# Roots by one GpSimd power with later users, and keys split for two head pairs at once, in a hybrid attention encoder

## The chip, the cores and the metric

The kernel runs on one core of one Trainium2 chip. A core has a matrix engine (TensorE, PE in the profile, with its weight loads as PEld), three engines for elementwise work (VectorE as DVE, ScalarE as ACT, GpSimd as POOL), and SyncE (SP), whose queue issues the DMA transfers here. The metric is the time of one launch in device microseconds (us); lower is better.

## What is computed

Two request groups (prompt and sample, 2048 tokens each, model width 1024, all in float32) pass through one encoder layer with the same weights:

```python
h = rms_norm(x, norm_w)
q_a, k_a, v_a, g_a, q_b, k_b, v_b, g_b = split(h @ w_in)   # 512|128|128|512|512|512|512|512
q_a, k_a = partial_rope(rms_norm(q_a, q_norm_a)), partial_rope(rms_norm(k_a, k_norm_a))
o_a = windowed_gqa_sink(q_a, k_a, v_a, sink_a) * silu(g_a)           # +-128 tokens, 8 query and 2 key heads of 64
q_b, k_b = rms_norm(q_b, q_norm_b), rms_norm(k_b, k_norm_b)
o_b = neighbourhood_attn(q_b, k_b, v_b, rpb_b) * silu(g_b)           # 8 x 16 window on a 64-wide grid, 8 heads
x = x + concat([o_a, o_b]) @ w_out
y = x + (p @ w_ple) * sigmoid(x @ w_ple_gate)
```

`rms_norm(x, g)` is `x * rsqrt(mean(x * x) + 1e-6) * g`. For the queries and keys the mean is taken over the 64 entries of a head, so a tile of 128 tokens with eight heads needs eight inverse square roots per token.

## The kernel before

Products in float32 are split into a high and a low part, each rounded for TensorE (`fp32r`), and formed as three matmuls (high x high, high x low, low x high). The splits follow one pattern: ScalarE writes the high part, VectorE (or GpSimd) subtracts it from the source and writes the low part.

There are three stages.

1. The first stage, tiles f = 0 to 31 (16 tiles of 128 tokens for each of the two request groups): `proj_a` projects group A's columns (`pk` for keys and values, 24 matmuls of 256 columns; `pq` for queries and `pg` for gates, 24 matmuls of 512 columns each); `unit_a` does the windowed attention of a tile, for each of the two key heads.
2. The second stage, f = 32 to 95, in two halves of 32 tiles: `proj_b` projects one half of group B's heads (four of eight) for one tile of a group (`pqk` for queries and keys, `pvg` for values and gates, 24 matmuls each); `unit_b` does the neighbourhood attention of four heads.
3. The third stage: the output projection, the residual, and the gated product with `p`.

`PLAN_A` and `PLAN_B` write out by hand at what fraction of a tile's projection work the pieces of the attention (scores `sc`, transposes of the probabilities `pt`, products with the values `po`, the end `fin`, the next tile's queries `prep`) stand between the projection's matmuls. The order of TensorE's instructions is pinned to this program order (`pinned`). On the other engines a planner orders the instructions, by program order as priority and by its own estimate of when an operand is ready; instructions inside `P(...)` keep their place. Each engine then takes its queue strictly in that order. In the loops of the projections, an index `i` counts the matmuls of one projection, and constants such as `PC = 6` (`roots` at matmul 6 of `pq`), `PV = 15` (`values`), `KA = 33` and `KB = 23` (`keys_a`, `keys_b`) say behind which matmul a piece is issued. The weights of TensorE lie in tiles `wa0` to `wa7` and `wb0` to `wb7`, which are loaded and split anew (L159, L160) at the change from the first to the second stage and between the second stage's halves.

What the change touches:

- `rsqrt` (L135) writes `y = v ** -0.5` for a tile `v` of n columns: two integer instructions for a first guess (L138, L140) and three Newton steps of three instructions (L143 to L145), all on VectorE. Its users: `roots` in `proj_a` (L459 to L466, n = 3: two key heads and the token's own root), the queries' part of `proj_a` (L488 to L494, n = 8), `proj_b` (L673 to L680, n = 8), and `stats_b` (twice, n = 16).
- The users of the roots: L464 scales the keys `kt` and L466 applies the rope to them with four GpSimd instructions (L451 to L454); L492 and L494 do the same for the queries `q`; L679 scales keys (`kb`) and queries (`qg`) of the second stage. `values` (L443) and the gate's tanh (L506) use the token's root as well.
- `keys_b` (L636) takes the transposed keys of four heads from PSUM, `pkt`, and splits them into `ks_b[0]` and `ks_b[1]`, one tile for each pair of heads; the high part of the pair's first head lies in partitions 0 to 63 and its low part in 64 to 127, and the other way round for the second. The scale `wk[:, 1:2]` (the product of the two norms' weights, over 8) is applied there. `prep_b` splits the queries without a scale, and `sc` in `unit_b` reads both.

Of the kernel before, what the change touches and what calls it, by code (L numbers as in the profile page):

```python
# [13 lines left out]
I32 = mybir.dt.int32  # L14
# [8 lines left out]
HD = 64  # L23
# [53 lines left out]
PC = 6  # L77
PB = (26, 30)
# [20 lines left out]
def emit(ctx, tc, io):  # L99
# [35 lines left out]
    def rsqrt(pool, v, y, n, tag):  # L135
        i2 = pool.tile([128, n], I32, tag=tag + "i", name=tag + "i")
        a = pool.tile([128, n], F32, tag=tag + "a", name=tag + "a")
        nc.vector.tensor_scalar(out=i2, in0=v.bitcast(I32), scalar1=1, scalar2=None,  # L138
                                op0=ALU.logical_shift_right)
        nc.vector.tensor_scalar(out=y.bitcast(I32), in0=i2, scalar1=-1, scalar2=0x5F3759DF,  # L140
                                op0=ALU.mult, op1=ALU.add)
        for _ in range(3):
            nc.vector.scalar_tensor_tensor(out=a, in0=y, scalar=-0.5, in1=y, op0=ALU.mult, op1=ALU.mult)  # L143
            nc.vector.tensor_tensor(out=a, in0=a, in1=v, op=ALU.mult)
            nc.vector.scalar_tensor_tensor(out=y, in0=a, scalar=1.5, in1=y, op0=ALU.add, op1=ALU.mult)  # L145
# [184 lines left out]
    def big(shape, dt, name):  # L330
        return ap.tile(shape, dt, tag="big", name=name, bufs=3)
# [89 lines left out]
    def proj_a(f):  # L421
# [35 lines left out]
        def roots():  # L457
# [4 lines left out]
            rsqrt(ap, vr[:, 8:11], y[:, 8:11], 3, "rqk")  # L462
# [4 lines left out]
        if f < 2:  # L467
            roots()
        yield 0, False
        pq = ptile([128, 512], "pj", "pq")  # L470
        for i, c in enumerate(project(pq, xr, lambda k, b: w_q[k][:, b, :], 215)):
            if i - 4 in HN and f in last:
                square(f + 1, HN[i - 4])
            if i == PC and f > 1:
                roots()
            if i == PV:
                values()
# [5 lines left out]
            if i == ka:  # L483
# [6 lines left out]
        rsqrt(ap, vr[:, 0:8], y[:, 0:8], 8, "rqa")  # L490
        q = ap.tile([128, 8, HD], F32, tag="qg", name="q", bufs=6)
        nc.vector.tensor_tensor(out=q, in0=pq.rearrange("p (h d) -> p h d", d=HD),  # L492
                                in1=y[:, 0:8].unsqueeze(2).broadcast_to([128, 8, HD]), op=ALU.mult)
        rope(q, 8, 0)  # L494
        yield 0, False
        pg = ptile([128, 512], "sc" if f == 1 else "pj", "pg")
        for i, c in enumerate(project(pg, xr, lambda k, b: w_g[k][:, b, :], 215)):
            if i in HG and f > 0 and not early:
                split(f + 1, HG[i])
            if i in HN and f > 0 and f not in last:  # L500
                square(f + 1, HN[i])
            yield c
# [54 lines left out]
    def stats_b(s):  # L557
# [4 lines left out]
        rsqrt(ap, ms_b[:, c], rs_b[:, c], NT, "rsb")  # L562
# [73 lines left out]
    def keys_b(kt, b, cb):  # L636
# [3 lines left out]
        for i in range(2):  # L640
            for e in range(2):
                a, z = 64 * e, 64 - 64 * e
                hi, lo = (ks_b[i][p:p + 64, 8 * b:8 * b + 8, e, 16 * cb:16 * cb + 16].rearrange("p r c -> p c r")
                          for p in (a, z))
                nc.scalar.activation(hi, pkt[a:a + 64, i], AF.Copy, scale=wk[a:a + 64, 1:2])  # L645
                nc.vector.scalar_tensor_tensor(out=lo, in0=pkt[a:a + 64, i], scalar=wk[a:a + 64, 1:2],  # L646
                                               in1=hi.bitcast(F32), op0=ALU.mult, op1=ALU.subtract)

    def proj_b(f):
# [5 lines left out]
        if not ks_b:  # L655
            ks_b.extend(big([128, 32, 2, 64], F32R, f"ks_b{i}") for i in range(2))
# [18 lines left out]
        rsqrt(ap, vr, y, 8, "rqb")  # L675
        qg = ap.tile([128, 2, 4, HD], F32, tag="qg", name="qg", bufs=6)
        kt = ap.tile([128, 4, HD], F32, tag="kt", name="kb", bufs=2)
        for dst, c in ((kt, 4), (qg[:, 0], 0)):
            nc.vector.tensor_tensor(out=dst, in0=pk[:, 64 * c:64 * c + 256].rearrange("p (h d) -> p h d", d=HD),  # L679
                                    in1=y[:, c:c + 4].unsqueeze(2).broadcast_to([128, 4, HD]), op=ALU.mult)  # L680
# [28 lines left out]
    def prep_b(f):  # L709
# [6 lines left out]
        for e in range(2):  # L716
            a, z = 64 * e, 64 - 64 * e
            nc.scalar.copy(q1[e][a:a + 64], pqt[a:a + 64])
            nc.vector.tensor_tensor(out=q2[e][a:a + 64], in0=pqt[a:a + 64], in1=q1[e][a:a + 64].bitcast(F32),
# [530 lines left out]
```

## Time and profile before

| | before |
|---|---|
| median of 3 runs | 2525.07 us (2524.78 to 2525.31) |
| the profiled execution | 2525.68 us, of which the span from first to last instruction is 2523.8 us |
| mean granted TensorE clock | 0.996 of full speed |
| busy time | PE 2478.9, PEld 2090.0, DVE 1948.5, ACT 1445.0, POOL 582.5 us |
| chain that ended last | PE 86%, DVE 6%, DMA 3%, ACT 3% |

Times in the views are in us from the span's start unless marked ns. A row of a stretch (`700.00:900.00 200.00, ...`) has, for each of PE, PEld, DVE, ACT and POOL, the busy time and in brackets the number of instructions, then the granted clock of PE (1.00 is full speed), the share of DMA engines in use and GB/s. A row of a group has line, engine, operation, what it writes and reads, the shapes, the count, then total busy us and mean ns of one, then the engine's idle time before these instructions and what ended it. A row of the timeline has start, duration, engine, line and operation, and in square brackets the idle time before it and the instruction that ended it. A row of the chain of waits has start, length, engine, what was written, and line. The first stage ends near 785 us, the second near 1870, the third takes the rest.

### The profile page before, as it was taken

Reading aid. Unit: us, or ns where it says so; the run is one execution under the profiler, and the core shown is the slowest. Engines: PE = TensorE matmul, PEld = TensorE weight load, DVE = VectorE, ACT = ScalarE, POOL = GpSimd, SP = SyncE. Lnnn points to the kernel's source line nnn. Section 1 sums busy time; section 2 is a strip of 40 time slices with the busy share of each in tenths; the row PEclk is TensorE's granted clock in tenths of the full one; section 3 lists DMA queues with packets and bytes.
Section 4 is the critical chain, followed back from the end, with each engine's and each line's share of the span. In section 5 each row is a group of like instructions: output and inputs, shape, how many; then the busy total and the mean of one; then the engine's idle time right before and its main releaser. Section 6 shows DMA issues by size and latency. Waiting matters only on the chain.

```text
span 2523.8 us, 41360 instructions
## 1 busy us (share of the span) xinstructions
PE 2478.9 (98%) x12912; PEld 2090.0 (83%) x12912; DVE 1948.5 (77%) x5860; ACT 1445.0 (57%) x3469; POOL 582.5 (23%) x873
## 2 busy tenths in 40 slices
PE   8999999999989999999999999999999999999998
PEld 7888888888877888888788888888787888888887
DVE  7888888888887777787888777787746655687776
ACT  6666666666665566666666666666864222354433
POOL 3333233323323333333333333332110000000000
PEclk9999999999999999999999999999999999999999
DMA  5333332211143555555755655455867455756764
GB/s 200 98 102 109 108 88 95 64 53 62 57 101 121 167 171 177 183 166 167 235 160 180 191 160 168 147 158 185 267 230 265 160 181 171 266 176 221 235 228 154
DMA packets 236044, 405.40 MB, mean 161 GB/s; under 512 B 30864, under 2 KB 85264, under 8 KB 230416
## 3 DMA queue, kind: packets, MB, share of 16 engines
q1 hardware_dynamic: 235824, 402.75, 50.0%
q8 instruction: 103, 1.69, 0.3%
q14 instruction: 117, 0.96, 0.1%
HBM read 297.79 MB, written 122.70 MB: 167 GB/s over the span
## 4 chain that ended last, share of the span: by engine, by line
PE 86%; DVE 6%; DMA 3%; ACT 3%; issue 1%; POOL 0%; SPq 0%; DVEq 0%; ACTq 0%; POOLq 0%
PE pqk L212 13%; PE pvg L212 13%; PE acca L1082 12%; PE accc L1082 9%; PE pq L212 6%; PE pg L212 6%; PE scb L212 3%; PE ptb L215 3%; PE pob L212 3%; PE sc L212 3%; PE pk L212 3%; PE po L212 3%; PE pt L215 3%; PE pple L212 3%; ACT s L243 1%
## 5 line engine op out<-in xcount | busy, mean ns | idle before, releaser
L243 ACT ACTIVATE s<-s,nm 128x384 f32<-128x384 f32 (+4 forms) x512 | 307.3, 601 | 341.9 <-DVE nm L238 213.9
L212 PE MATMUL pvg<-wb,xr 128*128 128x512 f32 x1536 | 462.0, 408 | 0.0
L212 PE MATMUL pqk<-wa,xr 128*128 128x512 f32 x1536 | 444.7, 412 | 0.0
L212 PEld LDWEIGHTS pqk<-wa,xr 128*128 128x128 f32 x1536 | 267.7, 190 | 37.7
L212 PEld LDWEIGHTS pvg<-wb,xr 128*128 128x128 f32 x1536 | 268.4, 190 | 31.5
L308 POOL TENSOR_TENSOR xr<-stx,xr 128x512 fp32r<-128x512 f32 x190 | 245.1, 1297 | 187.0 <-ACT xr L307 180.4
L1064 ACT CAST opd<-raw 128x512 fp32r<-128x512 f32 x224 | 131.2, 619 | 261.8 <-PE acca L1082 112.8
L1065 DVE TENSOR_TENSOR opd<-raw,opd 128x512 fp32r<-128x512 f32 x224 | 146.3, 685 | 111.8 <-ACT opd L1064 111.8
L212 PE MATMUL pg<-wb,xr 128*128 128x512 f32 x768 | 231.8, 409 | 0.0
L212 PE MATMUL pq<-wa,xr 128*128 128x512 f32 x768 | 219.9, 400 | 2.2 <-DVE wa L160 1.6
L1082 PE MATMUL accc<-opd,wb 128*128 128x512 f32 x768 | 177.0, 389 | 1.9 <-DVE r L1126 1.9
L1082 PE MATMUL acca<-opd,wa 128*128 128x512 f32 x768 | 175.9, 389 | 0.4 <-DVE opd L1065 0.4
L1082 PE MATMUL acca<-opd,s 128*128 128x512 f32 x768 | 175.8, 389 | 0.2 <-DVE opd L1065 0.2
L798 POOL TENSOR_TENSOR o_tb<-otb 128x256 f32<-128x256 f32 x64 | 48.1, 751 | 547.2 <-DVE otb L791 466.8
L1082 PEld LDWEIGHTS accc<-opd,wb 128*128 128x128 f32 x768 | 144.1, 188 | 32.2 <-DVE r L1126 2.3
L1082 PEld LDWEIGHTS acca<-opd,wa 128*128 128x128 f32 x768 | 144.0, 188 | 30.9 <-DVE opd L1065 0.9
L1082 PEld LDWEIGHTS acca<-opd,s 128*128 128x128 f32 x768 | 144.0, 188 | 30.7 <-DVE opd L1065 0.9
L212 PEld LDWEIGHTS pq<-wa,xr 128*128 128x128 f32 x768 | 139.1, 188 | 25.5 <-DVE wa L160 3.3
L212 PEld LDWEIGHTS pob<-p_t,vw 128*128 128x128 f32 (+2 forms) x832 | 133.0, 190 | 30.9 <-DVE p_t L772 6.4
L227 DVE CUSTOM_DVE_ANT_0 s<-scb,bias 128x288 f32<-128x288 f32 (+3 forms) x256 | 141.3, 553 | 18.8 <-PE scb L212 15.8
L212 PEld LDWEIGHTS pg<-wb,xr 128*128 128x128 f32 x768 | 137.8, 189 | 20.4
L646 DVE SCALAR_TENSOR_TENSOR ks_b<-pktb,wk,ks_b 64x128 fp32r<-64x128 f32 x256 | 115.1, 450 | 43.9 <-ACT ks_b L645 33.4
(170 smaller groups left out, 5256.0 us busy)
## 6 DMA issues: line engine op xcount, KB each, us to landing
stx<-x_b SPq DMA_DIRECT2D x128, 256.0 KB
vw<-v_d SPq DMA_DIRECT2D x112, 256.0 KB
stx<-x_a SPq DMA_DIRECT2D x64, 256.0 KB
stn<-x_n SPq DMA_DIRECT2D x64, 256.0 KB
v_d<-vb SPq DMA_DIRECT2D x64, 256.0 KB
ple_d<-ev SPq DMA_DIRECT2D x64, 256.0 KB
xres<-x_r SPq DMA_DIRECT2D x64, 256.0 KB
x_d<-r SPq DMA_DIRECT2D x64, 256.0 KB
```

The costliest lines, as they stand in the source:

```text
L212: pinned(nc.tensor.matmul(out, lhsT, rhs, start=start, stop=stop))
L215: pinned(nc.tensor.transpose(out, in_, eye))
L227: nc.vector.tensor_tensor_reduce(out=s[:, :n], in0=ps[:, :n], in1=bias, scale=1.0, scalar=-3.0e38, op0=ALU.add, op1=ALU.max, accum_out=sm[ ...
L243: ex = nc.scalar.activation(ss[i][:, :n], ss[i][:, :n], AF.Exp, bias=nm[:, i:i + 1], accum_out=den[:, i:i + 1])
L308: low.tensor_tensor(out=lo, in0=raw, in1=hi.bitcast(F32), op=ALU.subtract)
L646: nc.vector.scalar_tensor_tensor(out=lo, in0=pkt[a:a + 64, i], scalar=wk[a:a + 64, 1:2], in1=hi.bitcast(F32), op0=ALU.mult, op1=ALU.subtract)
L798: nc.gpsimd.tensor_tensor(out=o_t, in0=got["ot"][:, :, 0], in1=got["ot"][:, :, 1], op=ALU.add)
L1064: P(nc.scalar.copy(hi, v))
L1065: P(nc.vector.tensor_tensor(out=lo, in0=v, in1=hi.bitcast(F32), op=ALU.subtract))
L1082: pinned(nc.tensor.matmul(ps, w[k][:, a, c:c + 128], o[:, b], start=i in (0, 1, 4) and k == 0 and j == 0, stop=k == 3 and j == 2, skip_gro ...
```

## The change

`rsqrt` becomes one GpSimd instruction, a power with the exponent -0.5 from a constant tile. The instructions that use the roots move into functions of their own, which are issued later in the tile: the first stage's keys 7 matmuls behind the roots (`PW`), the first stage's queries and the second stage's keys and queries at matmul 10 of the next projection (`PR`; at matmul 1 for the last but one tile of a stretch, `last`). In the first two tiles they stay directly behind the roots. In the second stage, `ks_b` is ordered by the head's place in its pair instead of by pair, so that one copy and one subtraction split that head's keys of both pairs; the scale moves from the keys to the queries in `prep_b`.

```diff
+PW = 7
+PR = 10
...
-    def rsqrt(pool, v, y, n, tag):
-        i2 = pool.tile([128, n], I32, tag=tag + "i", name=tag + "i")
-        a = pool.tile([128, n], F32, tag=tag + "a", name=tag + "a")
-        nc.vector.tensor_scalar(out=i2, in0=v.bitcast(I32), scalar1=1, scalar2=None,
-                                op0=ALU.logical_shift_right)
-        nc.vector.tensor_scalar(out=y.bitcast(I32), in0=i2, scalar1=-1, scalar2=0x5F3759DF,
-                                op0=ALU.mult, op1=ALU.add)
-        for _ in range(3):
-            nc.vector.scalar_tensor_tensor(out=a, in0=y, scalar=-0.5, in1=y, op0=ALU.mult, op1=ALU.mult)
-            nc.vector.tensor_tensor(out=a, in0=a, in1=v, op=ALU.mult)
-            nc.vector.scalar_tensor_tensor(out=y, in0=a, scalar=1.5, in1=y, op0=ALU.add, op1=ALU.mult)
+    power = cp.tile([128, 1], F32, tag="power", name="power")
+    nc.vector.memset(power, -0.5)
+
+    def rsqrt(v, y, n):
+
+        nc.gpsimd.tensor_tensor(out=y, in0=v, in1=power.broadcast_to([128, n]), op=ALU.pow)
...
-            rsqrt(ap, vr[:, 8:11], y[:, 8:11], 3, "rqk")
+            rsqrt(vr[:, 8:11], y[:, 8:11], 3)
+
+        def keys():
+
             nc.vector.tensor_scalar_mul(y[:, 11:12], y[:, 10:11], 0.5)
             nc.vector.tensor_tensor(out=kt[:, 0:2, :], in0=pk[:, 0:128].rearrange("p (h d) -> p h d", d=HD),
                                     in1=y[:, 8:10].unsqueeze(2).broadcast_to([128, 2, HD]), op=ALU.mult)
             rope(kt[:, 0:2, :], 2, 1)
         if f < 2:
             roots()
+            keys()
...
             if i == PC and f > 1:
                 roots()
+            if i == PC + PW and f > 1:
+                keys()
...
-        rsqrt(ap, vr[:, 0:8], y[:, 0:8], 8, "rqa")
+        rsqrt(vr[:, 0:8], y[:, 0:8], 8)
         q = ap.tile([128, 8, HD], F32, tag="qg", name="q", bufs=6)
-        nc.vector.tensor_tensor(out=q, in0=pq.rearrange("p (h d) -> p h d", d=HD),
-                                in1=y[:, 0:8].unsqueeze(2).broadcast_to([128, 8, HD]), op=ALU.mult)
-        rope(q, 8, 0)
+
+        def queries():
+
+            nc.vector.tensor_tensor(out=q, in0=pq.rearrange("p (h d) -> p h d", d=HD),
+                                    in1=y[:, 0:8].unsqueeze(2).broadcast_to([128, 8, HD]), op=ALU.mult)
+            rope(q, 8, 0)
+        if f < 2:
+            queries()
...
+            if i == PR and f > 1:
+                queries()
...
-        for i in range(2):
-            for e in range(2):
-                a, z = 64 * e, 64 - 64 * e
-                hi, lo = (ks_b[i][p:p + 64, 8 * b:8 * b + 8, e, 16 * cb:16 * cb + 16].rearrange("p r c -> p c r")
-                          for p in (a, z))
-                nc.scalar.activation(hi, pkt[a:a + 64, i], AF.Copy, scale=wk[a:a + 64, 1:2])
-                nc.vector.scalar_tensor_tensor(out=lo, in0=pkt[a:a + 64, i], scalar=wk[a:a + 64, 1:2],
-                                               in1=hi.bitcast(F32), op0=ALU.mult, op1=ALU.subtract)
+        for e in range(2):
+            a, z = 64 * e, 64 - 64 * e
+            hi, lo = (ks_b[e][p:p + 64, 8 * b:8 * b + 8, :, 16 * cb:16 * cb + 16].rearrange("p r i c -> p i c r")
+                      for p in (a, z))
+            nc.scalar.copy(hi, pkt[a:a + 64])
+            nc.vector.tensor_tensor(out=lo, in0=pkt[a:a + 64], in1=hi.bitcast(F32), op=ALU.subtract)
...
-        rsqrt(ap, vr, y, 8, "rqb")
+        rsqrt(vr, y, 8)
...
-        for dst, c in ((kt, 4), (qg[:, 0], 0)):
-            nc.vector.tensor_tensor(out=dst, in0=pk[:, 64 * c:64 * c + 256].rearrange("p (h d) -> p h d", d=HD),
-                                    in1=y[:, c:c + 4].unsqueeze(2).broadcast_to([128, 4, HD]), op=ALU.mult)
+        def normed():
+
+            for dst, c in ((kt, 4), (qg[:, 0], 0)):
+                nc.vector.tensor_tensor(out=dst, in0=pk[:, 64 * c:64 * c + 256].rearrange("p (h d) -> p h d", d=HD),
+                                        in1=y[:, c:c + 4].unsqueeze(2).broadcast_to([128, 4, HD]), op=ALU.mult)
...
+            if i == (PR if f not in last else 1):
+                normed()
             yield c
...
-            nc.scalar.copy(q1[e][a:a + 64], pqt[a:a + 64])
-            nc.vector.tensor_tensor(out=q2[e][a:a + 64], in0=pqt[a:a + 64], in1=q1[e][a:a + 64].bitcast(F32),
-                                    op=ALU.subtract)
+            nc.scalar.activation(q1[e][a:a + 64], pqt[a:a + 64], AF.Copy, scale=wk[a:a + 64, 1:2])
+            nc.vector.scalar_tensor_tensor(out=q2[e][a:a + 64], in0=pqt[a:a + 64], scalar=wk[a:a + 64, 1:2],
+                                           in1=q1[e][a:a + 64].bitcast(F32), op0=ALU.mult, op1=ALU.subtract)
...
-                   ks_b[h // 2][:, r0:r0 + nr, h % 2, c0:c0 + ncol], j == 0, j == 1)
+                   ks_b[h % 2][:, r0:r0 + nr, h // 2, c0:c0 + ncol], j == 0, j == 1)
```

More of the change, by code (lines that the diff above doesn't have):

```diff
@@ L13 @@
 F32R = mybir.dt.float32r
-I32 = mybir.dt.int32
 AF = mybir.ActivationFunctionType
@@ L561, in stats_b @@
         nc.vector.tensor_scalar(out=ms_b[:, c], in0=ms_b[:, c], scalar1=EPS, scalar2=None, op0=ALU.add)
-        rsqrt(ap, ms_b[:, c], rs_b[:, c], NT, "rsb")
+        rsqrt(ms_b[:, c], rs_b[:, c], NT)
         nc.vector.tensor_scalar_mul(hr_b[:, c], rs_b[:, c], 0.5)
@@ L655, in proj_b @@
         if not ks_b:
-            ks_b.extend(big([128, 32, 2, 64], F32R, f"ks_b{i}") for i in range(2))
+            ks_b.extend(big([128, 32, 2, 64], F32R, f"ks_b{e}") for e in range(2))
         w_qk, w_vg = w_b[half]
```

## The prediction

> **What bounds the kernel now.** I read the page first (engine shares, then the chain that ended last), then the busy time of each engine in stretches of some 200 us.
>
> ```profile
> span 2523.8 us, 41360 instructions
> PE 2478.9 (98%) x12912; PEld 2090.0 (83%) x12912; DVE 1948.5 (77%) x5860; ACT 1445.0 (57%) x3469; POOL 582.5 (23%) x873
> PE 86%; DVE 6%; DMA 3%; ACT 3%; issue 1%; POOL 0%; SPq 0%; DVEq 0%; ACTq 0%; POOLq 0%
> 0.00:100.00 100.00, 90.30 (x483) 77.15 (x484) 80.65 (x297) 64.20 (x159) 32.76 (x68) 1.00 0.47 158
> 100.00:300.00 200.00, 200.00 (x1158) 176.03 (x1157) 172.56 (x659) 135.35 (x363) 64.77 (x121) 1.00 0.33 107
> 700.00:900.00 200.00, 190.08 (x944) 155.59 (x943) 154.55 (x508) 119.04 (x287) 60.75 (x73) 0.97 0.46 134
> 900.00:1100.00 200.00, 200.00 (x1094) 168.05 (x1092) 158.18 (x514) 125.02 (x306) 66.93 (x80) 1.00 0.55 172
> 1100.00:1300.00 200.00, 193.22 (x1033) 161.17 (x1032) 160.74 (x485) 130.32 (x310) 67.39 (x80) 0.98 0.61 192
> 1700.00:1900.00 200.00, 194.22 (x1032) 160.74 (x1031) 129.36 (x361) 136.57 (x313) 33.51 (x49) 1.00 0.69 225
> ```
>
> PE (TensorE) is busy for 2478.9 of 2523.8 us and makes 86% of the chain. The stretches say where the other 44.9 us lie. In the middle of the first stage (100 to 300 us) and of the second (900 to 1100 us) PE is busy in all 200.00 us: there nothing that VectorE (DVE), ScalarE (ACT) or GpSimd (POOL) does faster can move the end. PE stands idle at the start (9.70 us), at the change from first to second stage (9.92 us of 700 to 900), at the second stage's change of weights (6.78 us of 1100 to 1300) and at its end (5.78 us of 1700 to 1900), 32.2 us together. The first and the third row of these four also hold a clock of 0.97 and 0.98, so PE's work is slower there as well. What the change can win lies in these places, about 22 us of idle time behind 700 us and a little at the start. Two finer stretches and five waits of PE show who is late there.
>
> ```profile
> 720.00:730.00 10.00, 5.80 (x30) 4.28 (x28) 9.91 (x17) 7.06 (x14) 2.61 (x2) 0.86 0.75 237
> 730.00:740.00 10.00, 9.93 (x41) 8.26 (x42) 5.64 (x19) 6.79 (x17) 2.17 (x3) 0.79 0.23 64
> 726.64 0.62 PE L212 MATMUL sc<-ks_a,q 128*128 128x384 f32 x2 [1.75 <-DVE pr L605]
> 730.08 1.01 PE L212 MATMUL sc<-ks_a,q 128*128 128x384 f32 x2 [2.52 <-DVE mx L227]
> 1256.86 1.11 PE L212 MATMUL pob<-p_t,vw 128*128 128x256 f32 x4 [3.29 <-DVE q L719]
> 1274.78 0.66 PE L215 MATMUL ptb<-rowwise,s 128*128 128x128 f32 x4 [1.33 <-ACT s L243]
> 1780.31 0.67 PE L212 MATMUL pob<-p_t,vw 128*128 128x256 f32 x4 [1.10 <-DVE q L719]
> ```
>
> From 720 to 730 us PE works 5.80 us while VectorE works 9.91 us: the new weights are split on VectorE, and the scores (`sc`) wait 1.75 and 2.52 us for it. The clock then falls to 0.86 and 0.79. At 1256.86, 1274.78 and 1780.31 the waits (3.29, 1.33 and 1.10 us) end on VectorE's `q`, on ScalarE's exponentials and on `q` again. So VectorE's queue is the second limit, in a few places only.
>
> **The roots: what goes.** Each root is a chain of eleven VectorE instructions (two on integers, three times three of Newton). The groups of its middle instruction carry the price of all:
>
> ```profile
> L144 DVE TENSOR_TENSOR rqba<-rqba,vrb 128x8 f32<-128x8 f32 x192 | 32.0, 166 | 5.2
> L144 DVE TENSOR_TENSOR rqaa<-rqaa,vr 128x8 f32<-128x8 f32 x96 | 17.2, 179 | 1.2
> L144 DVE TENSOR_TENSOR rqka<-rqka,vr 128x3 f32<-128x3 f32 x96 | 15.4, 161 | 3.0
> ```
>
> Ninety-six and 192 are three per root, so there are 64 roots `rqb`, 32 `rqa` and 32 `rqk`. That is 11 x (64 x 0.166 + 32 x 0.179 + 32 x 0.161) = 237 us of 1948.5 us of VectorE, 12%, nearly all in the first 1765 us. In the full stretches this is hidden behind PE and worth nothing.
>
> **The roots: what comes.** 130 powers on POOL, on 3, 8 or (twice) 16 columns. No row shows a power. The nearest rows are products on POOL and one longer pass.
>
> ```profile
> L451 POOL TENSOR_TENSOR r<-q,tab 128x128 f32<-128x128 f32 x32 | 14.8, 463 | 248.3 <-DVE q L492 243.7 <-DVE den L252 4.6
> L453 POOL TENSOR_TENSOR r<-kt,tab 128x16 f32<-128x16 f32 x32 | 7.2, 224 | 0.0
> L798 POOL TENSOR_TENSOR o_tb<-otb 128x256 f32<-128x256 f32 x64 | 48.1, 751 | 547.2 <-DVE otb L791 466.8 <-issue 80.4
> ```
>
> A product takes 224 ns on 16 columns and 463 ns on 128: 2.1 ns a column on some 190 ns. The lower bound of a power is thus 0.21 us; it can't be below nothing, as an instruction is added. If a power is eleven passes as on VectorE, each an instruction of 224 ns, it is 2.5 us: my upper bound from rows. The ends are a factor of twelve apart; the nearest row is the short product (same engine and kind, few columns), but a power needs more steps per column, so I take their geometric mean, 0.7 us. 130 x 0.7 = 91 us on POOL, which is busy 582.5 us (23%): there is room.
>
> A rule that speaks against the change stands in the Trainium skill, GPSIMD Engine Reference, section "Performance versus the Vector engine": the same elementwise work is about twice as slow on GpSimd, and VectorE is the place for it. By that rule a root would be an estimated 2 x 1.9 = 3.8 us on POOL and the sum would come out slower, near 2550. The rows here agree only in part: POOL's 16 columns at 224 ns stand against 8 on VectorE at 166 ns, and the rule speaks of the same steps, which a power needn't be.
>
> **The users, and the wait that is added.** `kt`, `q`, `kb` and `qg` now wait on VectorE for POOL. Behind them in VectorE's queue stand the score sums, the splits of `p_t` and `pr`, and PE waits for those. What time a power has is seen in one tile of each stage.
>
> ```profile
> 207.67 0.23 DVE L459 TENSOR_SCALAR vr<-ssq,ee 128x2 f32<-128x2 f32 x1
> 210.28 0.29 DVE L464 TENSOR_TENSOR kt<-pk,y 128x128 f32<-128x128 f32 x1
> 191.59 0.22 DVE L488 TENSOR_SCALAR vr<-ssq,ee 128x8 f32<-128x8 f32 x1
> 196.85 0.69 DVE L492 TENSOR_TENSOR q<-pq,y 128x512 f32<-128x512 f32 x1
> 193.36 0.48 PE L212 MATMUL pg<-wb,xr 128*128 128x512 f32 x1
> 934.03 0.23 DVE L673 TENSOR_SCALAR vrb<-ssqb,ep_b 128x8 f32<-128x8 f32 x1
> 937.48 0.43 DVE L679 TENSOR_TENSOR kb<-pqk,yb 128x256 f32<-128x256 f32 x1
> 939.02 0.76 POOL L798 TENSOR_TENSOR o_tb<-otb 128x256 f32<-128x256 f32 x1 [9.36 <-DVE otb L791]
> ```
>
> First stage, keys: the variance is ready at 207.90 and the chain lets `kt` start at 210.28, so 2.4 us are free before anything is later than now. First stage, queries: ready at 191.81, `q` starts at 196.85; the eleventh matmul of `pg` (the new place) starts at 193.36, and the 1.9 us of chain that are gone from the queue pay for a wait up to about 195.2, so 3.4 us. Second stage: ready at 934.26, `kb` starts at 937.48, so 3.2 us. POOL is idle for 9.36 us before 939.02, so the power doesn't queue there. At 0.7 us, even at 2.3 us, nobody is late. `qg` moves up from behind the gate's product to the place of `kb`; both finish earlier than now. The rope's four POOL instructions move with their user by at most 3 us, past one product of the gate on POOL's queue, and its transposes come a tile later; no DMA moves, so SP's queue stays. For the first two tiles the users stand right behind the power: four powers of 0.7 us take the place of chains of 1.9 us.
>
> **The keys split for both pairs.** Per tile four ACT and four VectorE instructions on 64x128 become two of each on 64x256, without the scale; the queries' split takes the scale instead.
>
> ```profile
> L645 ACT ACTIVATE ks_b<-pktb,wk 64x128 fp32r<-64x128 f32 x256 | 124.8, 487 | 30.2 <-DVE ks_b L646 24.2 <-PE pktb L215 4.3
> L646 DVE SCALAR_TENSOR_TENSOR ks_b<-pktb,wk,ks_b 64x128 fp32r<-64x128 f32 x256 | 115.1, 450 | 43.9 <-ACT ks_b L645 33.4
> L718 ACT CAST q1b<-pqtb 64x256 fp32r<-64x256 f32 x128 | 46.1, 360 | 47.0 <-DVE q L719 44.8 <-PE pqtb L215 2.0
> L719 DVE TENSOR_TENSOR q<-pqtb,q1b 64x256 fp32r<-64x256 f32 x128 | 53.6, 419 | 3.4 <-ACT q1b L718 1.2
> L694 ACT ACTIVATE vb<-pvg,rs_b 128x256 fp32r<-128x256 f32 x64 | 30.5, 477 | 17.9 <-PE pvg L212 17.8
> ```
>
> The plain 64x256 forms take 360 (L718) and 419 ns (L719), but write in a row; L645 and L646 write strided. A merged one costs between 360 and 2 x 487 ns on ACT, between 419 and 2 x 450 ns on VectorE; I take the middle, 0.67 and 0.66 us, so each pair saves 0.30 and 0.24 us. The scale costs a query's split about 477 - 360 = 0.12 us on ACT (L694 has one, at the same 256 columns); I take as much for VectorE. Over 128 of each: ACT 23 us less (bounds 64 less, 15 more), VectorE 15 us less (bounds 46 less, 15 more). The scores' matmuls read `ks_b` in the same row stride as before, so PE's work stays.
>
> **The sum.** Only the places with idle PE count. Here the chain of waits, in order of time, is needed for the change of stages (first and last of seventeen pieces of root chains between them, 2.0 us in all, and the weights behind), then PE's first wait and the exponentials' last input near 1273.
>
> ```profile
> 701.94 0.07 DVE rqaa L143
> 714.52 0.09 DVE y L145
> 714.92 4.35 DMA wa<-w_in_c
> 5.87 1.96 PE L212 MATMUL pk<-wx,xr 128*128 128x256 f32 x6 [5.87 <-ACT wx L159]
> 1273.14 0.73 DVE L238 TENSOR_SCALAR nm<-mx 128x4 f32<-128x4 f32 x1
> ```
>
> - Start: of the 9.70 us the first weights hold 5.87, which stay. The first two tiles lose four chains; of the other 3.8 us I give them 1 us.
> - First to second stage: the 2.0 us of root chains on the path go, and the transfer of the weights, which begins behind them, comes earlier; the splits behind it stay. With a shorter stall the clock falls less, about 1 us: 3 us.
> - Change of weights near 1250: the exponentials before 1274.78 wait for `nm` at 1273.14, in front of which seven instructions of a root chain lie between weight splits: of 7 x 0.166 = 1.2 us I count 0.8, since neighbours overlap; merged keys and the earlier `qg` take about 1.2 us from the wait of 3.29 us and its neighbours, the clock 0.5 us: 2.5 us.
> - End of the second stage: merged keys and `qg`, 1 us.
> - Elsewhere 0; the last 600 us hold no root.
>
> 1 + 3 + 2.5 + 1 = 7.5 us. The profiled execution took 2525.68 us (span 2523.8 and 1.9 around it), 0.6 us above the median of 2525.07. 2525.07 - 7.5 = 2517.6, say 2518. A measurement of this kernel spreads by 0.02%; I count a change of under 0.2% (5 us) as none.
>
> **The rivals.**
> *Nothing moves.* PE's stalls are set by weights that land late (the chain ends them with DMA and weight splits), so VectorE's free time lies elsewhere. For it: most of the 12% is in stretches with 200.00 us of PE. Against: VectorE is at 9.91 of 10 us in the worst one. Time: 2525, between 2521 and 2529. Chance 0.22.
>
> *The power is longer than its gap.* VectorE takes its queue in order; a power of 8 columns above 3.2 us makes it stand, and PE after it. At 4.0 us a second-stage tile loses up to 4.0 - 3.2 = 0.8 us, 64 x 0.8 = 51 us, and a first-stage tile 4.0 - 3.4 = 0.6, 32 x 0.6 = 19 us; the power on 3 columns is shorter, 0.19 + 3/8 x 3.8 = 1.6 us, and stays under its 2.4. Half of these 70 us are absorbed, since VectorE has 20% idle time: 2525 + 35 = 2560; at 3.5 us only some 10 us are left, at 6 us over 100. For it: no row bounds a power from above with certainty, and each column may be worked out in software. Against: 2.5 us for eleven separate passes is still under the gap. Chance 0.28. The Trainium skill's rule on GpSimd, above, points to this rival.
>
> **How the numbers follow.** The forecast has 0.50; its own range is 2511 (stalls and clock dips nearly gone) to 2524 (1 us won). Three quarters of it lie below 2520, the rest within 0.2%. Faster: 0.50 x 0.75 + 0.02 of the first rival = 0.40. Same: 0.125 + 0.18 + the short end of the second rival = 0.31. Slower: 0.29, nearly all of it the second rival. The range 2511 to 2550 holds the forecast but for its tail, the first rival and some 40% of the second, 0.8 together.
>
> **What would show it.** Right: POOL shows 130 powers of under 2.4 us; VectorE's busy time falls by 230 to 290 us; few waits of `kt`, `q`, `kb` for POOL; PE's busy share in 700 to 900 rises and the clock there stays above 0.97; 100 to 300 and 900 to 1100 keep 200.00. Wrong: powers above 3 us with VectorE waiting for them in every tile (second rival), or the same idle time of PE at the same weight splits (first rival). A new order of VectorE's queue, which a planner writes, could also shift single waits by a few us either way; that is in the ranges.

## The result, and the profile after

| | before | after |
|---|---|---|
| median | 2525.19 us (2524.78 to 2529.02, 4 runs) | 2593.98 us (2591.05 to 2594.53, 4 runs) |
| the profiled execution | 2525.68 us | 2594.49 us, span 2592.7 us |
| mean granted TensorE clock | 0.996 | 0.994 |

The changed kernel is slower: its time is 1.0267 times that of before, 95% interval 1.0249 to 1.0284. That lies outside the forecast's range (2511 to 2550). First the page and the stretches of the changed kernel (for each engine the busy time and the number of instructions):

```profile
span 2592.7 us, 39712 instructions
PE 2506.2 (97%) x12912; PEld 2086.1 (80%) x12912; DVE 1731.8 (67%) x4303; ACT 1412.8 (54%) x3341; POOL 774.8 (30%) x1003
PE 56%; DVE 13%; ACT 9%; POOL 8%; issue 7%; DMA 6%; SPq 0%; POOLq 0%; DVEq 0%; ACTq 0%
0.00:100.00 100.00, 85.61 (x441) 72.82 (x441) 61.49 (x183) 58.30 (x141) 42.58 (x71) 0.95 0.47 156
100.00:300.00 200.00, 193.09 (x1098) 167.13 (x1097) 144.67 (x445) 129.98 (x351) 80.91 (x134) 1.00 0.30 96
700.00:900.00 200.00, 192.51 (x980) 159.00 (x979) 134.28 (x362) 116.71 (x285) 80.67 (x93) 0.99 0.41 119
900.00:1100.00 200.00, 193.91 (x1036) 157.66 (x1036) 125.52 (x327) 115.12 (x272) 87.53 (x92) 1.00 0.55 169
```

VectorE (DVE) lost 217 us of work, and still the two stretches that were full have gaps: 193.09 and 193.91 of 200 us. The number of matmuls tells it more clearly than the busy share. From 100 to 300 us there are 1098 where there were 1158; 5.2% fewer, worth 10.4 us of that stretch. From 900 to 1100 there are 1036 where there were 1094. VectorE has 13% of the chain (before 6%) and GpSimd (POOL) 8% (before nothing). The groups and waits name the cause (the waits have total us, times, longest):

```profile
L141 POOL TENSOR_TENSOR yb<-vrb,power 128x8 f32<-128x8 f32 x64 | 106.1, 1658 | 212.7 <-DVE vrb L680 199.7
L141 POOL TENSOR_TENSOR y<-vr,power 128x8 f32<-128x8 f32 x32 | 52.8, 1651 | 106.9 <-DVE vr L490 106.9
L141 POOL TENSOR_TENSOR y<-vr,power 128x3 f32<-128x3 f32 x32 | 27.6, 862 | 71.1 <-DVE vr L455 71.1
DVE kb L688 <- POOL yb L141: 80.9, 61, 1.8
DVE q L497 <- POOL y L141: 35.7, 29, 2.7
DVE y L462 <- POOL y L141: 32.1, 31, 1.3
PE sc L208 <- DVE mx L223: 25.0, 28, 1.9
PE pob L208 <- DVE p_t L783: 18.4, 55, 0.8
```

The row of the kernel before for the same wait for score maxima:

```profile
PE sc L212 <- DVE mx L227: 4.6, 5, 2.5
```

A power takes 1.65 us on 8 columns and 0.86 us on 3, under the gaps of 3.2, 3.4 and 2.4 us that the prediction read. Even so VectorE stands 149 us for it, in nearly every tile, and TensorE waits for score maxima (`mx`, 25.0 us; before 4.6) and split probabilities (`p_t`, 18.4 us; before 2.4). The two timelines of VectorE's queue around a root show how that fits together. The first is before, behind the queries' variance that ends at 191.81 us and the second stage's that ends at 934.26:

```profile
192.39 0.55 DVE L227 CUSTOM_DVE_ANT_0 s<-sc,mask 128x384 f32<-128x384 f32 x1
194.21 0.16 DVE L145 SCALAR_TENSOR_TENSOR y<-rqaa,y 128x8 f32<-128x8 f32 x1
195.57 0.56 DVE L227 CUSTOM_DVE_ANT_0 s<-sc,mask 128x384 f32<-128x384 f32 x1
...
935.78 0.17 DVE L143 SCALAR_TENSOR_TENSOR rqba<-yb 128x8 f32<-128x8 f32 x1
935.87 0.68 DVE L227 CUSTOM_DVE_ANT_0 s<-scb,bias 128x512 f32<-128x512 f32 x1
936.59 0.17 DVE L238 TENSOR_SCALAR nm<-mx 128x4 f32<-128x4 f32 x1
```

The second shows the changed kernel: a later tile of the first stage with the same shapes, and the same tile of the second stage:

```profile
400.09 0.22 DVE L490 TENSOR_SCALAR vr<-ssq,ee 128x8 f32<-128x8 f32 x1
400.40 1.65 POOL L141 TENSOR_TENSOR y<-vr,power 128x8 f32<-128x8 f32 x1 [3.43 <-DVE vr L490]
402.08 0.69 DVE L497 TENSOR_TENSOR q<-pq,y 128x512 f32<-128x512 f32 x1 [1.17 <-POOL y L141]
402.69 0.55 DVE L223 CUSTOM_DVE_ANT_0 s<-sc,mask 128x384 f32<-128x384 f32 x1
403.30 0.61 PE L208 MATMUL sc<-ks_a,q 128*128 128x384 f32 x2 [0.82 <-DVE mx L223]
404.96 0.56 DVE L223 CUSTOM_DVE_ANT_0 s<-sc,mask 128x384 f32<-128x384 f32 x1
...
968.90 0.23 DVE L680 TENSOR_SCALAR vrb<-ssqb,ep_b 128x8 f32<-128x8 f32 x1
970.89 0.42 DVE L688 TENSOR_TENSOR kb<-pqk,yb 128x256 f32<-128x256 f32 x1 [1.16 <-POOL yb L141]
971.23 0.68 DVE L223 CUSTOM_DVE_ANT_0 s<-scb,bias 128x512 f32<-128x512 f32 x1
971.96 0.17 DVE L234 TENSOR_SCALAR nm<-mx 128x4 f32<-128x4 f32 x1
```

Before, the gap was not empty. The planner had woven the score sums (L227) between the eleven instructions of the chain: in the first stage the first sum began 0.58 us behind the variance and the fourth 3.76 us, in the second stage the fourth sum 1.61 us and the negated maximum `nm` 2.33 us. After the change there is nothing to weave into: `q` or `kb` stands in the queue ahead of sums, VectorE waits idle at it, and the sums behind it (four in the first stage, the fourth in the second) wait as well. In the first stage the first sum now begins 2.38 us behind the variance (402.69 - 400.31) and the fourth 4.65 us, 1.8 and 0.9 us later than before. TensorE waits 0.82 us at 403.30. In the second stage the fourth sum begins 2.10 and `nm` 2.83 us behind the variance, 0.5 us later each. This tile is a mild one: over the 55 tiles of the second stage in which two sums follow the variance, the median place of `nm` moves from 1.87 to 2.67 us behind it. And the users stand directly behind the root although they are issued seven and ten matmuls later, since the planner places what is not pinned by its own estimate of when an operand is ready.

### The profile page after: what moved, and what is told of

Read it like the earlier page. It is cut to its first block, busy times and chain, and to the rows that moved or that the text cites. A ratio compares the mean times of both kernels' runs of the same rounds, so it can differ in the third digit from the quotient of the medians.

```text
span 2592.7 us, 39712 instructions
## 1 busy us (share of the span) xinstructions
PE 2506.2 (97%) x12912; PEld 2086.1 (80%) x12912; DVE 1731.8 (67%) x4303; ACT 1412.8 (54%) x3341; POOL 774.8 (30%) x1003
## 4 chain that ended last, share of the span: by engine, by line
PE 56%; DVE 13%; ACT 9%; POOL 8%; issue 7%; DMA 6%; SPq 0%; POOLq 0%; DVEq 0%; ACTq 0%
PE acca L1093 12%; PE accc L1093 9%; PE pq L208 6%; PE pvg L208 4%; PE pqk L208 4%; PE pg L208 4%; PE pk L208 3%; PE po L208 3%; PE pple L208 3%; POOL yb L141 2%; PE sc L208 2%; ACT s L239 2%; PE pt L211 2%; POOL xr L304 2%; POOL y L141 2%
## 5 line engine op out<-in xcount | busy, mean ns | idle before, releaser
L141 POOL TENSOR_TENSOR yb<-vrb,power 128x8 f32<-128x8 f32 x64 | 106.1, 1658 | 212.7 <-DVE vrb L680 199.7
L208 PE MATMUL pob<-p_t,vw 128*128 128x256 f32 (+7 forms) x832 | 133.2, 273 | 27.5 <-DVE p_t L783 18.4
L802 DVE TENSOR_TENSOR otb<-pob,otb 64x512 f32<-64x512 f32 x128 | 88.1, 688 | 100.4 <-ACT otb L801 97.5
```

The lines of the kernel that those rows point to most:

```text
L141: nc.gpsimd.tensor_tensor(out=y, in0=v, in1=power.broadcast_to([128, n]), op=ALU.pow)
L208: pinned(nc.tensor.matmul(out, lhsT, rhs, start=start, stop=stop))
L802: nc.vector.tensor_tensor(out=ot[a:a + 64], in0=pq[a:a + 64], in1=ot[a:a + 64], op=ALU.add)
```

## The experiments

**Theory 1 (T1):** VectorE stands in its queue for the power, with score sums behind it. **Rivals:** the new splits cost (T2), or GpSimd's load and what it shares (T3). All ratios are to the kernel before, measured beside each run; the brackets are 95% intervals.

**The parts.** The first run has the new split of keys alone, the second all but it, the third VectorE's chain again under the later users and the new split.

```diff
 # e1_keys_only: kernel before, and of the change only keys_b, prep_b and the operand of sc
-                nc.scalar.activation(hi, pkt[a:a + 64, i], AF.Copy, scale=wk[a:a + 64, 1:2])
+            nc.scalar.copy(hi, pkt[a:a + 64])
...
 # e2_no_keys: changed kernel, and these hunks undone
...
 # e8_chain_late: changed kernel, rsqrt with the eleven VectorE instructions of before
-        nc.gpsimd.tensor_tensor(out=y, in0=v, in1=power.broadcast_to([128, n]), op=ALU.pow)
+        nc.vector.tensor_scalar(out=i2, in0=v.bitcast(I32), scalar1=1, scalar2=None, ...
```

> The kernel before with only the second stage's keys split for both pairs at once (and the scale moved to the queries); the roots stay on VectorE. Theory 1 (the loss is VectorE standing in its queue for the power, 1.0 to 1.3 us at each of 128 roots, with the score sums behind it): 2520, between 2515 and 2527, since this part has no power. Theory 2 (the loss comes from the longer split of the queries and the new shapes of the key split in the second stage): 2555 or more. Theory 3 (the loss comes from POOL's 192 us of powers, which hold POOL and the SBUF interface that it shares with VectorE): 2525.

> The changed kernel with the key split as it was before; powers and later users stay. Theory 1: 2595 to 2602, as slow as the changed kernel or a little slower, with 1.0 to 1.3 us of VectorE's idle time before each kb, q and kt. Theory 2: about 2555, half of the loss gone. Theory 3: 2595.

> The changed kernel with its roots by VectorE's chain of eleven instructions again; the later users and the new split of keys stay. Theory 1 (only the wait for the power costs): as with the split of keys alone, 2531 us (2524 to 2536), and VectorE's busy time near 1950 us. Rival (the moved users cost by themselves, since the second stage's queries now stand ahead of the score sums): 2540 us or more.

Measured: 1.0016 (1.0006 to 1.0025), 2531.42 us; 1.0210 (1.0194 to 1.0225), 2580.93 us; and 1.0012 (1.0003 to 1.0021), 2532.23 us. The power with its users makes 2.1 of the 2.67%. The split alone is slightly slower where T1 expected 2515 to 2527, and without it the changed kernel is faster than T1's 2595 to 2602: two misses with one reason, T1 had taken the split as free. It makes 4 us by itself and about 14 on top of the powers (2.67% against 2.10%), so T2 has a small part of the loss.

**The price of the root.** A product in place of the power (the roots are then not computed), and a second power ahead of each.

```diff
 # e4_cheap_root
-        nc.gpsimd.tensor_tensor(out=y, in0=v, in1=power.broadcast_to([128, n]), op=ALU.pow)
+        nc.gpsimd.tensor_tensor(out=y, in0=v, in1=power.broadcast_to([128, n]), op=ALU.mult)
 # e6_double
+        nc.gpsimd.tensor_tensor(out=extra, in0=v, in1=power.broadcast_to([128, n]), op=ALU.pow)
         nc.gpsimd.tensor_tensor(out=y, in0=v, in1=power.broadcast_to([128, n]), op=ALU.pow)
```

> The changed kernel with a product in place of the power (same operands, same engine, same place in the queue; the roots' values are not computed). Theory 1: the wait falls with the instruction's time, 1.65 to about 0.2 us: 2515 to 2530. Theory 2: 2590. Theory 3: 2525 as well, as POOL's busy time falls by some 165 us; e3 tells 1 from 3.

> The changed kernel with one more power of the same columns, written to a tile that nobody reads, ahead of each power. Theory 1 (the length of the power is what VectorE stands for): between a product of 0.2 us and the power of 1.65 us the time rose by 77 us for 1.45 us, 53 us for each us; a second power makes the wait 1.65 us longer, so some 88 us more, 2680 us (2650 to 2720), less if VectorE's spare time is not used up, and the waits of kb for POOL go from 1.3 to 3 us each. Rival (what costs is that an instruction of another engine stands in the chain at all, whatever its length): under 2610 us. Rival (the load on GpSimd and what it shares): the rise is as large in the stretches in which no user waits.

Measured: 0.9961 (0.9949 to 0.9974), 2516.88 us; and 1.0962 (1.0944 to 1.0981), 2773.56 us. The product's group and two stretches of its kernel, then the powers and two of TensorE's waits in the doubled one:

```profile
L141 POOL TENSOR_TENSOR yb<-vrb,power 128x8 f32<-128x8 f32 x64 | 13.8, 216 | 230.6 <-DVE vrb L680 220.7 <-DMA stx<-x_b 4.5 <-DMA raw<-w_out 3.1
100.00:300.00 200.00, 200.00 (x1161) 175.64 (x1160) 150.45 (x462) 136.36 (x364) 65.83 (x136) 1.00 0.33 105
900.00:1100.00 200.00, 200.00 (x1097) 168.04 (x1095) 131.27 (x345) 121.04 (x286) 71.05 (x95) 1.00 0.58 177
```

```profile
L144 POOL TENSOR_TENSOR yb<-vrb,power 128x8 f32<-128x8 f32 x64 | 104.9, 1639 | 0.0
PE sc L211 <- DVE mx L226: 64.1, 29, 2.5
PE ptb L214 <- ACT s L242: 63.5, 57, 1.5
100.00:300.00 200.00, 182.95 (x977) 157.96 (x976) 127.64 (x403) 115.97 (x311) 90.86 (x134) 0.94 0.27 86
1500.00:1700.00 200.00, 180.75 (x953) 145.13 (x952) 116.91 (x308) 106.35 (x253) 94.55 (x95) 1.00 0.51 156
```

With a root of 0.2 us both stretches are full again, and the kernel beats the one before: the same order of work on VectorE, ScalarE and GpSimd, the same number of GpSimd instructions, only shorter. From there to the power, 96 roots grow by 1.44 us and 32 by 0.67, 160 us in all, and the time by 3.06%, 77 us: half is absorbed. The second power adds 1.64 and about 0.85 us, 185 us, and the time grows by 6.95%, 176 us: 95% arrives at the end. Part of the second rise is TensorE's clock, 0.94 to 0.95 from 100 to 700 us, where the changed kernel had 1.00. The second stage, with 0.98 to 1.00 from 900 us on, is the cleaner measure: from its first `pqk` matmul to its last it takes 1016.5 us with the product, 1060.1 with one power and 1154.4 with two, so 47% of the first power's 92 us arrive there and 90% of the second's 105. The expected 2680 (2650 to 2720) was too low, because it went on with the first slope, when the slack was mostly used up, and because of the clock. In 57 of 64 second-stage tiles TensorE now waits for the exponentials `s`, which wait for `nm`, behind the fourth sum, behind `kb`.

**The place in the queue.** The changed kernel with users issued at once (both distances 0), then with users pinned to their written places, then pinned and with the old split.

```diff
 # e5_early
-PW = 7
-PR = 10
+PW = 0
+PR = 0
 # e3_pinned (also q, kt and the factor at L462); e7_pinned_old_keys: the same with the old split of keys
-                nc.vector.tensor_tensor(out=dst, in0=pk[:, 64 * c:64 * c + 256].rearrange(...), ...)
+                P(nc.vector.tensor_tensor(out=dst, in0=pk[:, 64 * c:64 * c + 256].rearrange(...), ...))
```

> The changed kernel with both distances set to 0: each user is issued directly behind its root in program order, as before the change. Theory 1 (VectorE stands in its queue for the power, because the planner puts the users right behind the root whatever matmul they are issued at): VectorE's queue is nearly the same one, so 2594 us, within 8. Rival (the seven and ten matmuls do carry part of the wait): the waits of q, kt and kb for POOL grow beyond the 149 us they have in the changed kernel, and the time is 2605 us or more.

> The changed kernel with the users of the roots (the factor 0.5, kt, q, kb, qg) held in program order, which puts q and kb behind the tile's four score sums in VectorE's queue instead of between them; powers, places 7 and 10 and all work stay the same. Theory 1: most of the loss goes, 2520 to 2540, VectorE's idle time before kb and q falls from 117 us to under 20 us and PE's waits for mx (25 us) to under 5 us. Theory 2: 2590. Theory 3: 2590, as POOL does the same.

> The changed kernel with its users kept at their written places in VectorE's queue and with the split of keys of the kernel before. Theory 1 with the split as an own cost: pinned it was 2538 with the new split; the new split alone costs 4 us on the kernel before and 13 us on top of the powers, so 2525 to 2534. Rival (the rest of the pinned kernel's loss comes from the pinned users, which now hold up q and kb): stays at 2538, with PE still waiting for kb at the transposes.

Measured: 1.0285 (1.0270 to 1.0301), 2602.17 us; 1.0041 (1.0026 to 1.0056), 2538.30 us; 1.0027 (1.0017 to 1.0038), 2537.48 us. Without the seven and ten matmuls the time is the same within the intervals and the waits for GpSimd are 153 us in place of 149, so these distances did nearly nothing (T1 had 2594 within 8 us, its rival 2605 or more). Pinned, most of the loss is gone at the same powers: the waits of `kb` fall from 80.9 to 5.2 us, while GpSimd is busy as long as in the changed kernel (772.5 and 774.8 us). That refutes T3, which expected 2590. The old split gives back 0.14%, within the overlap of the two intervals: e7_pinned_old_keys lies outside the 2525 to 2534 of T1 and where its rival had it, and TensorE still waits 7.1 us for `kb` in ten tiles.

```profile
L141 POOL TENSOR_TENSOR yb<-vrb,power 128x8 f32<-128x8 f32 x64 | 106.0, 1657 | 237.0 <-DVE vrb L680 231.7
DVE kb L688 <- POOL yb L141: 5.2, 3, 1.7
```

**What the pinned kernel still lost.** The chain of eleven for the first two tiles and the 16 columns; and, beside it, two parts of the kernel before by themselves: a shorter chain, and only the scale moved to the queries.

```diff
 # e10_chain_start: e7_pinned_old_keys, and in rsqrt
+        if not late:                      # f < 2, and stats_b
+            return newton_root(v, y, n)   # the eleven VectorE instructions
 # e9_two_steps: kernel before
-        for _ in range(3):
+        for k, c in ((-0.5005962965370867, 1.5017504289868662), (-0.4995838204565647, 1.4995842805920157)):
 # e11_scale_on_queries: kernel before, prep_b of the change, and in keys_b
-                nc.scalar.activation(hi, pkt[a:a + 64, i], AF.Copy, scale=wk[a:a + 64, 1:2])
+                nc.scalar.copy(hi, pkt[a:a + 64, i])
```

> The changed kernel with pinned users and the old split of keys, and with VectorE's chain of eleven instructions for the roots of the first two tiles and for the two roots of 16 columns. Theory (what the pinned kernel still loses lies at the start, where users stand directly behind powers of 0.86 and 1.65 us and TensorE works 86.7 of the first 100 us instead of 90.3, at a clock of 0.95): the loss of 0.27% halves at least, to 0.00 to 0.13% above the kernel before, and the first 100 us have 90 us of TensorE again. Rival (the loss lies in the pinned order itself, at kb and the transposes of the keys behind it): still 0.2 to 0.3% above.

> The kernel before, with two Newton steps instead of three, their constants fitted to the first guess (the worst root is then off by 6 parts in ten million); nothing waits for another engine, no place moves. Eight VectorE instructions a root instead of eleven: 65 us less of VectorE. Theory 1 (VectorE's time counts only in the places where it is late; without any power, and with the new split of keys, 84 us less of the chain's instructions per 2517 gave 11 us): about 3/11 of what the product in place of the root won, 2 to 4 us under the kernel before. Rival (the forecast's first rival, nothing moves): within 1 us of it.

> The kernel before with the scale moved from the keys' split to the queries' split, and the keys still split pair by pair in four copies and four subtractions. It is one half of the new split of keys, which as a whole cost 0.16% and 0.12%. Theory (the longer queries' split, 0.47 and 0.48 us instead of 0.36 and 0.42, delays the scores' operands): the whole cost is here, 0.10 to 0.20% above the kernel before. Rival (the merged splits cost, being longer single instructions in front of others): within 0.05%.

Measured: 1.0011 (1.0002 to 1.0020), 2532.38 us; 0.9995 (0.9986 to 1.0004), 2526.03 us; 1.0006 (0.9997 to 1.0015), 2528.83 us. The start was part of the loss, though the intervals of 1.0027 and 1.0011 overlap a little: with the chain there TensorE works 89.87 of the first 100 us again, where the pinned kernel worked 86.70. Of the rest the profile shows one new wait:

```profile
0.00:100.00 100.00, 89.87 (x470) 76.42 (x471) 73.01 (x239) 62.33 (x154) 38.46 (x73) 0.97 0.47 157
PE pktb L226 <- DVE kb L705: 7.2, 10, 3.1
```

At matmul 10 the pinned `kb` stands behind the attention's end, too late for the transposes of the keys. The other two settle little: three instructions less per root take 55 us from VectorE and give 0.05%, within the interval, where 2 to 4 us (0.08 to 0.16%) were expected, and the scale's part lies between none and the whole of the split's cost. What makes the new split slower stays open.

**One place.** Two kernels that differ only in where the second stage's users are issued.

```diff
 # e10_chain_start, and in proj_b: e12_five with 5, e13_seven with 7
-            if i == (PR if f not in last else 1):
+            if i == (5 if f not in last else 1):
```

> The pinned kernel with the old split of keys and the chain of eleven for the first two tiles and the 16 columns, with the second stage's users (normed) at matmul 5 of the next projection instead of 10. That puts kb in VectorE's queue behind the third score sum and ahead of the fourth, as the changed kernel has it; the first stage stays pinned. Theory 1 (one place in the queue is the loss: the fourth score sum, the maximum's negation and the exponentials behind it stand behind a kb that waits for the power): the second stage's part of the loss comes back, some 0.7 us for each of 64 tiles less what the key split had in it, 25 to 45 us over the kernel before, with kb waiting some 1.3 us for POOL in every tile. Rival (the changed kernel lost through its whole new order, not by this place): within 10 us of the kernel before.

> The same kernel with normed at matmul 7: kb stands right behind the fourth score sum and the negated maximum, ahead of the products of the attention's end. Theory 1: the wait for POOL all but goes, as the power has ended by then (two score sums of 0.55 us lie between), and TensorE's waits for kb at the keys' transposes (7.2 us in ten tiles with matmul 10) go too; 0.0 to 0.3% faster than the kernel before, 2519 to 2527 us. Rival (a wait for another engine costs wherever it stands): slower than with matmul 10, over 0.15% above the kernel before.

Measured: 1.0070 (1.0057 to 1.0082), 2546.30 us; and 0.9974 (0.9965 to 0.9983), 2522.65 us against 2528.59 for the kernel before beside it. The first has `kb` ahead of the fourth score sum, the second right behind `nm`. The first is 17.7 us over the kernel before, less than the 25 to 45 us of its theory 1 and more than the 10 of its rival; the second lies where its theory 1 had it.

```profile
DVE kb L705 <- POOL yb L156: 73.8, 56, 1.8
1300.00:1500.00 200.00, 199.03 (x1067) 162.25 (x1066) 133.74 (x363) 124.34 (x308) 87.55 (x94) 1.00 0.56 172
```

```profile
1300.00:1500.00 200.00, 200.00 (x1095) 168.73 (x1094) 140.21 (x375) 127.76 (x318) 92.03 (x99) 1.00 0.58 179
1343.11 0.23 DVE L697 TENSOR_SCALAR vrb<-ssqb,ep_b 128x8 f32<-128x8 f32 x1
1343.42 1.64 POOL L156 TENSOR_TENSOR yb<-vrb,power 128x8 f32<-128x8 f32 x1 [3.80 <-DVE vrb L697]
1344.26 0.46 DVE L238 CUSTOM_DVE_ANT_0 s<-scb,bias 128x288 f32<-128x288 f32 x1 [0.56 <-PE scb L223]
1344.76 0.17 DVE L249 TENSOR_SCALAR nm<-mx 128x4 f32<-128x4 f32 x1
1345.10 0.42 DVE L705 TENSOR_TENSOR kb<-pqk,yb 128x256 f32<-128x256 f32 x1 [0.16 <-POOL yb L156]
```

One place in VectorE's queue is worth 0.96%, 24 us, or 0.38 us for each of 64 tiles. In the median tile `nm` begins 2.67 us behind the variance with matmul 5 and 1.61 with 7, so about a third of this delay arrives at the end. The busy share alone hides it: 199.03 against 200.00 us, but 1067 matmuls against 1095. With matmul 7, the last two score sums and `nm` stand where the wait was: `kb` waits 0.16 us in the tile above and 7.5 us in all tiles together (73.8 with matmul 5), and the attention's end comes behind it. Against matmul 10, where TensorE waits for the late `kb`, it is 0.37% (9 us). This kernel beats both others: 0.26% faster than before.

The traces tell the stages apart, since TensorE's order is pinned: the same matmul marks the same place in every kernel. The table has the start of the first matmul of `pqk` (the second stage's projection) and of `acca` (the third stage), in us from the span's start, one execution each.

| | before | e2_no_keys | e7_pinned_old_keys | e12_five | e13_seven |
|---|---|---|---|---|---|
| first `pqk` | 734.7 | 763.2 | 736.8 | 732.1 | 729.7 |
| first `acca` | 1902.6 | 1953.7 | 1911.5 | 1923.4 | 1897.8 |
| between them | 1167.9 | 1190.5 | 1174.7 | 1191.3 | 1168.1 |

Of the loss of e2_no_keys 28.5 us lie ahead of the second stage and 22.6 in it. Pinning, all that differs between it and e7_pinned_old_keys, gives back 26.4 us ahead of the second stage, so the users' place in the queue is the cause there too. In the second stage the one place ahead of the fourth sum makes the whole loss again (e12_five, 23.4 us), and the place behind `nm` none of it (0.2 us). What e13_seven wins, 5.0 us, lies ahead of the second stage. Two or three us of such differences are noise: e12_five and e13_seven have the same first stage and differ there by 2.4.

## Why the prediction was wrong

- *What bounds the kernel* held (though the clocks of 0.97 and 0.98 stand in the second and third of its four places, and its spread of 0.02% was that of three runs; with the fourth it is 0.17%). Roots of 0.2 us leave the middles of both stages full and win 0.39%, 10 us, where the sum over the idle places gave 7.5 us (e4_cheap_root).
- *The roots: what goes* held in its verdict, that it is worth nothing in the full stretches, and less in its size: VectorE fell by 217 us (230 to 290 forecast), 33 of them by the split (e8_chain_late has 1915.5 us), so 184 by the roots where the sum had 237. Instructions of the chain overlap their neighbours, as at 935.78 and 935.87, and a sum of durations counts that time twice.
- *The roots: what comes* was mis-sized. The geometric mean of 0.21 and 2.5 us gave 0.7 us; measured were 0.86 us (3 columns) and 1.65 us (8), inside the bounds. The rule of the Trainium skill (GPSIMD Engine Reference, "Performance versus the Vector engine") had led to an estimate of 3.8 us for a root; the trace does not agree with that estimate, since one power of 1.65 us is shorter than the chain of 11 x 0.166 = 1.8 us on VectorE. The rule itself, on the same operation on both engines, is not tested by a power in place of a chain. The rule pointed to the right sign, by a price that was not the one paid.
- *The users, and the wait that is added* is the step that failed, and it would have failed at the right price too: "At 0.7 us, even at 2.3 us, nobody is late" does not hold at 1.65 us. The gap was read as the time until the user ran, and the prediction named the score sums as queued behind it. It did not look at what VectorE did inside the gap. Between 191.81 and 196.85 it ran four score sums, `nm` and other work among the chain, and in the changed order the four sums come behind the user. It also trusted that the written distances of 7 and 10 matmuls would hold in VectorE's queue; e5_early shows that they don't. And `qg` did not move up: it still waits for the gate's product on GpSimd (36.1 us in 57 tiles, before 31.9 in 56).
- The rival *the power is longer than its gap* had the mechanism and the side right, and its guess that half would be absorbed came out near (149 us of waits, 69 us of time). Its point, 3.2 us, came from the same misread gap, and so its 2560 asked for a power of 4 us.
- *Start*: forecast 1 us won; instead TensorE works 85.61 us of the first 100 (before 90.30). Four more kernels with powers there have 86.2 to 86.7, six with the chain of eleven 89.5 to 90.6, so most of the loss comes with the power; not all of it is the power's length, since the kernel with the product has 88.62 and e9_two_steps 87.85. A power there queues on GpSimd behind the rope of the tile ahead, which the prediction did not count:

```profile
37.88 0.46 POOL L450 TENSOR_TENSOR q<-r 128x128 f32<-128x128 f32 x1
38.30 1.65 POOL L141 TENSOR_TENSOR y<-vr,power 128x8 f32<-128x8 f32 x1
39.98 0.69 DVE L497 TENSOR_TENSOR q<-pq,y 128x512 f32<-128x512 f32 x1 [2.71 <-POOL y L141]
```

- *First to second stage* held: 3 us were forecast, and from 700 to 900 us TensorE is busy for 192.51 us (before 190.08) at a clock of 0.99 (0.97). From the matmul that starts at 695.0 us in the kernel before to the one that starts there at 866.0, e13_seven takes 3.3 us less, e4_cheap_root 5.5 and e9_two_steps 3.9; e8_chain_late, with the chain, takes 0.1 more. The *change of weights* is less clear: from 1231.2 to 1318.3 us, e4_cheap_root takes 3.4 us less (2.5 forecast), but e8_chain_late takes 3.2 less as well, with the chain, so this need not come from the roots. In the changed kernel these gains stand beside the 70 us lost.
- *The keys split for both pairs* had its sizes right and its sign wrong:

```profile
L654 DVE TENSOR_TENSOR ks_b<-pktb,ks_b 64x256 fp32r<-64x256 f32 x128 | 79.8, 624 | 11.4 <-ACT ks_b L653 8.4
L653 ACT CAST ks_b<-pktb 64x256 fp32r<-64x256 f32 x128 | 78.5, 613 | 15.1 <-DVE ks_b L654 6.8 <-PE pktb L211 3.6
L730 DVE SCALAR_TENSOR_TENSOR q<-pqtb,wk,q1b 64x256 fp32r<-64x256 f32 x128 | 61.7, 482 | 8.5 <-ACT q1b L729 6.8
L729 ACT ACTIVATE q1b<-pqtb,wk 64x256 fp32r<-64x256 f32 x128 | 59.2, 462 | 45.6 <-DVE q L730 45.4
```

The merged splits take 0.61 and 0.62 us (0.67 and 0.66 taken), and the scale costs 0.10 and 0.06 us (0.12 taken). ACT works 32 us less. Counted as a gain near the weights, it costs 0.16% alone and 0.12% with the later users.

## What to carry to other kernels

When a wait is to replace work in an engine's queue, look at what that engine did between the operand and its user: other instructions woven into the old chain will stand behind the new wait, and a gap that is full of them is no gap. A later place in program order is not a later place in the queue if a planner reorders it, so read the order off the trace and, where it matters, pin the user right behind the last instruction that others wait for. In a stretch whose busy share looks full, count the matmuls.

## What the runs showed of the hardware

A power on GpSimd costs by the column, which was not expected from the products: 0.86, 1.65 and 2.91 us for 3, 8 and 16 columns (the last is the mean of `stats_b`'s two), about 0.16 us for each column and 0.4 us beside, an estimate from these three, while the product on the same 3 and 8 columns takes 0.20 and 0.21 us.

```profile
L141 POOL TENSOR_TENSOR rs_b<-ms_b,power 128x16 f32<-128x16 f32 x2 | 5.8, 2907 | 1.7 <-DVE es L245 1.4 <-DVE ms_b L570 0.3
```

TensorE's clock went with the length of its single waits here, not with their sum. In the doubled kernel (rows of e6_double above) it is idle for 17 of 200 us in the first stage, in seven waits of 2.44 us, and was granted 0.94; in the second stage it is idle for 19 us, in waits of at most 1.44 us, and was granted 1.00. No run varied this by itself.
